# Two transformer blocks on one core: GpSimd's part of the first block's mixer given to other engines, and late vectors loaded by another queue

## The chip, the cores and the metric

The program runs on one core of a Trainium2 chip. The metric is device time in microseconds (us) for one execution; the median of three runs of the kernel before is 3050.2 us (3048.06 to 3050.91). The engines are named as in the profile: PE is TensorE, DVE is VectorE, ACT is ScalarE, POOL is GpSimd, SP is SyncE; SPq and ACTq are the issues of DMAs by SP and ACT.

## The reference

Two blocks run one behind the other over x (256 tokens) and a context ctx (256 tokens) of 1024 columns, all in f32, each block with two layers. A layer of the first block is a feed-forward half step, a mixer, and another feed-forward half step, each behind an RMS norm whose shift and scale come from an adaLN product with c. The mixer, cut to what the change touches:

```python
q = rms_norm((rms_norm(q_lat, g_q_lat) @ w_q_up).reshape(b, n, 8, 96), g_q_head)
k = rms_norm(concat([k_nope, k_pe]), g_k_head)      # 64 + 32 columns a head
q, k = apply_rope(q, rope), apply_rope(k, rope)     # on the last 32; not for ctx
attn = softmax(q @ k.T * 96 ** -0.5) @ v            # x attends to x and ctx, ctx to ctx

u, v = split(gelu(sg_in)); v = rms_norm(v, g_sgu)   # 4 groups of 64 columns
sg = u * (einsum('gpq,bnqgc->bnpgc', w_spatial, v) + b_spatial)

cv = b_gate * conv3(c_gate * xin, w_conv)           # three taps along the tokens
h = h + gate * (concat([norm(attn), norm(sg), norm(cv)]) @ w_mix_out)
```

In layer 1, the last of the block, ctx needs keys and values alone. The second block's code is the same before and after.

## The kernel before, in words

Activations lie feature-major in SBUF: 128 features by 512 tokens, x as tokens 0 to 255 (stream 0), ctx as 256 to 511 (stream 1). Every weight is loaded as f32 by SP (`load_raw`, L301, tile `wr`, three buffers) and split into a high part by ACT (`wh`, L310) and a low part by DVE (`wl`, L311); activations are split in the same way (`xnh` by L593, `xnl` by L594; `gh`, `ysh` and others by L590, low parts by L591). A product is three matmuls, high by high, low by high, high by low (L340 to L342 feature-major, L354 to L356 token-major). A scheduler of the framework fixes the order of the instructions on each engine at build time; on the chip each engine then runs its own list in order and waits by semaphore.

**Start.** x and ctx are transposed to feature-major. `Sumsq.add` squares the eight tiles of a stream (ACT L95, L98) and sums them (DVE L100, the last by L103); PE sums over features (L548, psum `nm`), DVE makes the reciprocal root (L559 to L567), PE spreads it (L542). The first adaLN chunk is loaded by SP as eight tiles `ar` (L156, 1 MB each) in four parts; PE multiplies them (L167) and each part frees two of the eight feature tiles to be normed (DVE L133, ACT L593, DVE L594). `first_pair` of `ffn` multiplies them as they come (psum `fa`), so its four parts run one behind the other. The weights of the first pair are `wr_285` and `wr_293`, of the second `wr_655` and `wr_663`. After the second pair of layer 0, `load_vectors` is called for the vectors that are wanted later: 14 small DMAs into `rows` (L405), a transpose on PE (L409) and a copy to `cols` (L410). They are issued by ACT.

**Mixer 1** (`mixer1`). Constants come into one buffer `blk` by ACT's queue (L916 to L925): rope tables, the two head gains (broadcast to all partitions; the query's is scaled on POOL, L920), the gain `gsgu`, the bias `sgb`. Latents are projected and normed (`rms_split`; of its tiles every second low part is done by POOL, L591). Then come the gate's values `vg` (gelu, L878 to L883), the queries `qraw` and keys `kraw` (token-major, 128 tokens by 2 by 8 heads by 96), with sums of squares per head in `qss` and `kss` (16 columns each, two of either), and the shared rope part of the keys, which POOL copies to all heads (L1016). `head_scale` is called for each stream's queries and keys: a reciprocal root of 16 columns in eleven small DVE steps (L854, L527 to L531), a multiply by it (DVE L859), a multiply by the gain (POOL L860), and, for stream 0, rope per group of 128 tokens: L866, four small rotations L870 and L871, a sum L872. Beside this the projections for `yB` (gelu) and the short convolution (L1032, L1038 to L1041) run; `gating` transposes `w_spatial` (L1058, copied to `sg` by L1059) and norms `vg` (L1061 to L1070, its last two multiplies on POOL). POOL clears the unused 32 partitions of `qT` and `kT` (L1096). For each head PE then transposes keys and queries (L1101, psum `tr`), which ACT (L1103) and DVE (L1105) copy to `kT` and `qT`. Attention follows, in steps: scores (PE L804), maximum (DVE L810), exp (ACT L812), scaling (DVE L814, L815), transposes (PE L825) and values (L835).

## Time and profile before

| | us |
|---|---|
| median of 3 runs | 3050.2 |
| profiled execution, its own time | 3051.59 |
| its span | 3049.9 |
| PE busy | 2927.8 (96%) |
| DVE busy | 2151.0 (71%) |
| ACT busy | 1083.4 (36%) |
| POOL busy | 130.1 (4%) |
| mean granted clock of PE | 0.979 |

The profiled execution is a single one with its own time beside its span. Each instruction in it has a start and a length, and for idle time before it the profile names what ended the wait. PE's clock is a share of its full speed; it has two levels, 0.50 (1.2 GHz) and 1.00 (2.4 GHz), and a window shows the mean. Shares of the whole span average over stages with different limits, so the places around an edit are read by windows and by rows of single engines.

### The profile page before, as it was taken

To read this page: it belongs to the slowest core of one execution; us is meant where nothing else is said; L and a number is where in the kernel's file an instruction comes from. 1 tells how busy PE (TensorE), PEld (TensorE's weight loads), DVE (VectorE), ACT (ScalarE), POOL (GpSimd) and SP (SyncE) were. 2 spreads that over 40 slices of the span, in tenths; PEclk is the share of its full clock that TensorE was granted. 3 is DMA by queue.
4 is the path that set the end of the run, shared out by engine and by line. 5 is a ranking of instruction groups with operands and counts; after the bars stand their busy time and mean duration, and the time that the engine had idled before them with its cause. 6 is when DMAs were issued, how large, how long until landed. Compare 5 with 4: busy or idle time off the path is not lost.

```text
span 3049.9 us, 44489 instructions
## 1 busy us (share of the span) xinstructions
PE 2927.8 (96%) x17770; PEld 2489.2 (82%) x17770; DVE 2151.0 (71%) x4361; ACT 1083.4 (36%) x1977; POOL 130.1 (4%) x138
## 2 busy tenths in 40 slices
PE   5999999999999999999978999999999999999998
PEld 4788889678788888878857999886887879886998
DVE  4887868968887688877796575337688875536665
ACT  2222235443222232222544444235432223434443
POOL 0000001300000000000030000011000000011000
PEclk7999999999999999999989999999999999999999
DMA  6555533204655445554322554201245552312553
GB/s 224 171 193 185 174 100 95 75 15 157 203 193 165 152 138 188 185 193 145 101 93 70 182 182 136 74 7 53 80 156 174 186 189 62 113 51 69 164 180 111
DMA packets 357571, 410.52 MB, mean 135 GB/s; under 512 B 23774, under 2 KB 297844, under 8 KB 357364
## 3 DMA queue, kind: packets, MB, share of 16 engines
q1 hardware_dynamic: 353040, 403.48, 41.0%
q10 hardware_dynamic: 4324, 4.20, 0.4%
q8 instruction: 140, 2.29, 0.3%
q14 instruction: 67, 0.55, 0.1%
HBM read 406.60 MB, written 1.05 MB: 134 GB/s over the span
## 4 chain that ended last, share of the span: by engine, by line
PE 89%; DVE 7%; DMA 2%; ACT 1%; issue 1%; SPq 0%; POOL 0%; ACTq 0%; DVEq 0%; POOLq 0%
PE pj L340 13%; PE pj L341 12%; PE pj L342 12%; PE fa L340 9%; PE fa L341 9%; PE fa L342 9%; PE po L835 2%; PE pf L340 2%; PE pf L342 2%; PE pf L341 2%; PE sc L804 2%; DVE wl L311 2%; PE pt L825 1%; PE ada L483 1%; PE pj L354 1%; PE pj L355 1%
## 5 line engine op out<-in xcount | busy, mean ns | idle before, releaser
L310 ACT ACTIVATE wh<-wr 128x1024 fp32r<-128x1024 f32 (+3 forms) x542 | 525.9, 1017 | 877.1 <-PE pj L341 470.6
L311 DVE TENSOR_TENSOR wl<-wr,wh 128x1024 fp32r<-128x1024 f32 (+3 forms) x542 | 629.9, 1184 | 171.3 <-ACT wh L310 169.5
L472 DVE SCALAR_TENSOR_TENSOR ad<-wr,silu,ad 128x512 f32<-128x512 f32 x784 | 551.2, 750 | 16.5 <-DMA wr<-in_w_ada_dram 16.5
L340 PE MATMUL fa<-xnh,wh 128*128 128x512 f32 (+1 forms) x1472 | 519.6, 360 | 6.3 <-ACT xnh L593 4.5
L341 PE MATMUL fa<-xnl,wh 128*128 128x512 f32 (+1 forms) x1472 | 522.5, 357 | 2.0 <-DVE xnl L594 2.0
L342 PE MATMUL fa<-xnh,wl 128*128 128x512 f32 (+1 forms) x1472 | 522.6, 357 | 0.9 <-DVE wl L311 0.9
L340 PE MATMUL pj<-gh,wh 128*128 128x256 f32 (+1 forms) x1372 | 458.9, 336 | 0.0
L342 PE MATMUL pj<-gh,wl 128*128 128x256 f32 (+1 forms) x1372 | 456.8, 333 | 0.0
L341 PE MATMUL pj<-gl,wh 128*128 128x256 f32 (+1 forms) x1372 | 456.2, 333 | 0.0
L340 PEld LDWEIGHTS fa<-xnh,wh 128*128 128x128 f32 x1472 | 275.5, 189 | 53.2 <-issue 7.8
L342 PEld LDWEIGHTS fa<-xnh,wl 128*128 128x128 f32 x1472 | 277.8, 189 | 43.6 <-DVE wl L311 1.4
L341 PEld LDWEIGHTS fa<-xnl,wh 128*128 128x128 f32 x1472 | 277.5, 189 | 43.2 <-DVE xnl L594 3.2
L340 PEld LDWEIGHTS pj<-gh,wh 128*128 128x128 f32 x1372 | 258.6, 189 | 30.6 <-issue 4.0
L342 PEld LDWEIGHTS pj<-gh,wl 128*128 128x128 f32 x1372 | 258.2, 188 | 27.3
L341 PEld LDWEIGHTS pj<-gl,wh 128*128 128x128 f32 x1372 | 258.8, 189 | 26.2 <-issue 0.4
L341 PE MATMUL pj<-xnl,wh 128*128 128x256 f32 (+1 forms) x824 | 260.5, 320 | 1.2 <-DVE xnl L594 1.0
L340 PE MATMUL pj<-xnh,wh 128*128 128x256 f32 (+1 forms) x824 | 259.1, 324 | 2.4 <-ACT xnh L593 2.2
L342 PE MATMUL pj<-xnh,wl 128*128 128x256 f32 (+1 forms) x824 | 261.0, 320 | 0.0
L340 PEld LDWEIGHTS pj<-xnh,wh 128*128 128x128 f32 x824 | 155.1, 192 | 15.6 <-ACT xnh L593 3.2
L341 PEld LDWEIGHTS pj<-xnl,wh 128*128 128x128 f32 x824 | 156.6, 191 | 13.0 <-DVE xnl L594 1.7
L342 PEld LDWEIGHTS pj<-xnh,wl 128*128 128x128 f32 x824 | 156.3, 190 | 11.6
L686 DVE SCALAR_TENSOR_TENSOR h<-pj,gate,h 128x256 f32<-128x256 f32 x168 | 75.8, 481 | 99.2 <-PE pj L342 99.0
(373 smaller groups left out, 4387.9 us busy)
## 6 DMA issues: line engine op xcount, KB each, us to landing
wr<-in_w_ada_dram SPq DMA_DIRECT2D x112, 1024.0 KB, 5.2
wr<-in_w_ffn_in_dram SPq DMA_DIRECT2D x88, 1024.0 KB, 5.1
wr<-in_w_mlp_dram SPq DMA_DIRECT2D x64, 1024.0 KB, 5.5
...
```

The lines of the kernel that those rows point to most:

```text
L310: self.nc.scalar.activation(h[:, i0:i1], raw[:, i0:i1], AF.Copy)
L311: self.nc.vector.tensor_tensor(l[:, i0:i1], raw[:, i0:i1], h[:, i0:i1].bitcast(F32), op=ALU.subtract)
L340: nc.tensor.matmul(o, wh, x.H(k, c0, c1), start=st, stop=False)
L341: nc.tensor.matmul(o, wh, x.L(k, c0, c1), start=False, stop=False)
L342: nc.tensor.matmul(o, wl, x.H(k, c0, c1), start=False, stop=en)
L354: nc.tensor.matmul(ps_ap, xh, w.h[:, kw, n0:n1], start=st, stop=False)
L355: nc.tensor.matmul(ps_ap, xh, w.l[:, kw, n0:n1], start=False, stop=False)
L472: nc.vector.scalar_tensor_tensor(acc[:, j], raw[:, k - k0], s[:, k, j : j + 1], acc[:, j], op0=ALU.mult, op1=ALU.add)
L483: nc.tensor.matmul(ps[q : q + 32, :P], self.sumto[:, 3 - r : 35 - r], acc[:, j, o : o + P], start=(r == 0), stop=(r == 3), tile_position=( ...
L686: self.nc.vector.scalar_tensor_tensor(self.h[m][:, e0:e1], ps[:, e0 - c0 : e1 - c0], gate[:, m, s : s + 1], self.h[m][:, e0:e1], op0=ALU.m ...
L804: nc.tensor.matmul(ps[:, :w], q_ap(q0), k_ap(k0 * P, (k0 + nk) * P), start=True, stop=bias is None)
L835: nc.tensor.matmul(o, v_ap(k0 + k), pT[:, k, :], start=(k == 0), stop=(k == nk - 1), tile_position=(0, 64 * j))
```

## The change

It does four things. In `ffn`, the late vectors' DMAs are issued by SP instead of ACT, with `g_sgu` as one more of them. In `head_scale`, the gains go: those of the rope columns into tables made once per mixer (`head_table`), those of the other 64 into a column `gcol` by which the evacuations of the transposes multiply; all 16 (token group, head) pairs are done by one instruction, and the roots of both streams by one chain of 32 columns (`rms`). gelu leaves out its halving (`gelu2`, with the factors in `gsc`, `sgb` and the norm's mean). And POOL's remaining work in the mixer goes to DVE (low parts, the `vg` norm) or ACT (the copies of the rope part), or is no longer needed (the clearing; transposes now take 128 columns from a flat raw tile of 1568, and 128 partitions are evacuated). ACT also gets the convolution's first tap.

```diff
@@ setup, ffn @@
-             ("g_q_lat", a["g_q_lat"]), ("g_kv_lat", a["g_kv_lat"]), ("g_out", a["g_out"]), ("w_conv", a["w_conv"])],
+             ("g_q_lat", a["g_q_lat"]), ("g_kv_lat", a["g_kv_lat"]), ("g_out", a["g_out"]), ("w_conv", a["w_conv"]), ("g_sgu", a["g_sgu"])],
...
-                    self.load_vectors(2, len(self.groups), nc.scalar)
+                    self.load_vectors(2, len(self.groups), nc.sync)
@@ split_from, rms_split @@
-        eng = nc.gpsimd if pool else nc.vector
...
-            eng.tensor_tensor(l, t, h.bitcast(F32), op=ALU.subtract)
+            nc.vector.tensor_tensor(l, t, h.bitcast(F32), op=ALU.subtract)
...
-                self.split_from(u, dst, k0 + i, c0, c1, pool=i % 2 == 1)
+                self.split_from(u, dst, k0 + i, c0, c1)
@@ head_scale, head_table, gelu2: the new bodies @@
+    def head_scale(self, raw, y, tab):
+        v = self.nc.vector
+        r = raw.rearrange("p t h d -> p (t h) d")
+        v.tensor_tensor(r, r, y.unsqueeze(2).broadcast_to([P, 16, 96]), op=ALU.mult)
+        pe = raw[:, :, :, 64:96]
+        if len(tab.shape) == 2:
+            pe = r[:, :, 64:96]
+            v.tensor_tensor(pe, pe, tab.unsqueeze(1).broadcast_to([P, 16, 32]), op=ALU.mult)
+            return
...
+        v.tensor_tensor(t1, pe, tab[:, 0].unsqueeze(2).broadcast_to([P, 2, 8, 32]), op=ALU.mult)
         for t in range(2):
+            for o in (0, 8):
...
+                v.tensor_tensor(dst, src, sn.unsqueeze(1).broadcast_to([P, 8, 2, 8]), op=ALU.mult)
+        v.tensor_tensor(pe, t1, t2, op=ALU.add)
+    def head_table(self, tab, g):
+        v = self.nc.vector
+        v.tensor_tensor(tab[:, 0], self.cosq, g.unsqueeze(1).broadcast_to([P, 2, 32]), op=ALU.mult)
+        for t in range(2):
+            half = lambda ap, o: ap.rearrange("p (a b) -> p a b", b=16)[:, :, o : o + 8]
+            v.scalar_tensor_tensor(half(tab[:, 1, t], 0), half(self.sinq[:, t], 0), -1.0, half(g, 8), op0=ALU.mult, op1=ALU.mult)
+            v.tensor_tensor(half(tab[:, 1, t], 8), half(self.sinq[:, t], 8), half(g, 0), op=ALU.mult)
+    def gelu2(self, out, x_ps, w):
...
+        nc.scalar.activation(sq, x_ps, AF.Square, scale=float(np.sqrt(0.044715)))
+        nc.vector.scalar_tensor_tensor(sq, sq, 1.0, x_ps, op0=ALU.add, op1=ALU.mult)
         nc.scalar.activation(sq, sq, AF.Tanh, scale=float(np.sqrt(2.0 / np.pi)))
+        nc.vector.scalar_tensor_tensor(out, sq, 1.0, x_ps, op0=ALU.add, op1=ALU.mult)
@@ mixer1: constants @@
-        nc.gpsimd.tensor_scalar(gbc[:, 0:96], gbc[:, 0:96], 96 ** -0.5, None, op0=ALU.mult)
-        nc.scalar.dma_start(gsgu, a["g_sgu"][l].rearrange("g c -> (g c)").unsqueeze(0).broadcast_to([P, 256]))
+        for i, nm in enumerate(("g_q_head", "g_k_head")):
+            nc.scalar.dma_start(gcol[:64, i : i + 1], a[nm][l, 0:64].unsqueeze(1))
+        v.memset(gcol[64:96], 1.0)
+        v.memset(gcol[96:], 0.0)
+        v.tensor_scalar(gcol[:64, 0:1], gcol[:64, 0:1], 96 ** -0.5, None, op0=ALU.mult)
+        v.tensor_scalar(gbc[:, 64:96], gbc[:, 64:96], 96 ** -0.5, None, op0=ALU.mult)
+        for i in range(2):
+            self.head_table(tabs[i], gbc[:, 96 * i + 64 : 96 * i + 96])
+        v.tensor_scalar(gsc, self.vec("g_sgu", 2 * l, 2), 0.25, None, op0=ALU.mult)
...
+        v.tensor_scalar(sgb, sgb, 0.5, None, op0=ALU.mult)
@@ mixer1: heads @@
+            flat = self.arena([P, 1568], F32, name)
+            v.memset(flat[:, 1536:], 0.0)
...
+        def rms(ss, n):
+            v.tensor_scalar(ss[:, :n], ss[:, :n], 1.0 / 96, EPS, op0=ALU.mult, op1=ALU.add)
+            y = self.small(32, "hy")
+            self.rsqrt_small(y[:, :n], ss[:, :n], n)
...
-            nc.gpsimd.tensor_copy(kraw[tt // 2][:, tt % 2, :, 64:96], kpe[:, tt, :].unsqueeze(1).broadcast_to([P, 8, 32]))
+            nc.scalar.activation(kraw[tt // 2][:, tt % 2, :, 64:96], kpe[:, tt, :].unsqueeze(1).broadcast_to([P, 8, 32]), AF.Copy)
+        kst = kss.rearrange("p (t h) -> p t h", h=8)
+        v.tensor_tensor(kst, kst, pes.unsqueeze(2).broadcast_to([P, 4, 8]), op=ALU.add)
+        yq = rms(qss, 8 * nt)
+        yk = rms(kss, 32)
         for s in range(2):
             if s < len(streams):
-                self.head_scale(qraw[s], qss[s], gbc[:, 0:96], s == 0)
-            self.head_scale(kraw[s], kss[s], gbc[:, 96:192], s == 0)
+                self.head_scale(qraw[s], yq[:, 16 * s : 16 * s + 16], gbc[:, 64:96] if s else tabs[0])
+            self.head_scale(kraw[s], yk[:, 16 * s : 16 * s + 16], gbc[:, 160:192] if s else tabs[1])
@@ mixer1: convolution, gating, transposes @@
-            v.tensor_scalar(yy, zz, wc(1), None, op0=ALU.mult)
+            nc.scalar.activation(yy, zz, AF.Copy, scale=wc(1))
...
-            nc.gpsimd.tensor_tensor(vgs, vgs, yv[:, : nt * 4].unsqueeze(2).broadcast_to([P, nt * 4, 64]), op=ALU.mult)
-            nc.gpsimd.tensor_tensor(vg[:, :nt, :], vg[:, :nt, :], gsgu.unsqueeze(1).broadcast_to([P, nt, 256]), op=ALU.mult)
+            v.tensor_tensor(vgs, vgs, yv[:, : nt * 4].unsqueeze(2).broadcast_to([P, nt * 4, 64]), op=ALU.mult)
...
-        for t_ in qT + kT:
-            nc.gpsimd.memset(t_[96:, :, :], 0.0)
...
+                    nc.tensor.transpose(ps[:, tt * P : (tt + 1) * P], src[tt // 2][:, o : o + P], self.ident)
+                if src is kflat:
+                    nc.scalar.activation(dst[h // 4][:, h % 4, : n * P], ps[:, : n * P], AF.Copy, scale=gcol[:, 1:2])
                 else:
+                    v.tensor_scalar(dst[h // 4][:, h % 4, : n * P], ps[:, : n * P], gcol[:, 0:1], None, op0=ALU.mult)
```

Three places where the scheduler's order comes out otherwise follow. In rows of the changed kernel, line numbers are those of its own file; `sq` and `acc` are the squares and their sum, `h` the tiles of x and ctx.

The first is ACT at the start, among the squares; rows with a minus stood there before, rows with a plus stand there now.

```order
 L98 ACTIVATE sq_167<-h_97 128x256
-L405 DMA rows<-in_norm_g_dram 16x128 x2
-L405 DMA rows<-in_mlstm_norm_g_dram 8x128
 L98 ACTIVATE sq_211<-h_92 128x256
-L405 DMA rows<-in_final_g_dram 8x128
 L98 ACTIVATE sq_218<-h_93 128x256
 L98 ACTIVATE sq_225<-h_94 128x256
 L98 ACTIVATE sq_232<-h_95 128x256
-L310 ACTIVATE wh_287<-wr_285 128x1024 x2
 L98 ACTIVATE sq_239<-h_96 128x256
 L98 ACTIVATE sq_246<-h_97 128x256
```

The vectors' DMAs are gone from between ctx's squares (tiles `sq_211` to `sq_246`), and the split of the first weight, `wh_287`, now follows all of them. Somewhat later ACT's list has, now as before (where the line is L593), the tiles of part 1 of the first norm with the split of the second pair's weight among them:

```order
L592 ACTIVATE xnh_359<-nt_439,mod_104 128x256
L592 ACTIVATE xnh_359<-nt_443,mod_104 128x256
L592 ACTIVATE xnh_359<-nt_447,mod_104 128x256
L310 ACTIVATE wh_657<-wr_655 128x1024 x2
L592 ACTIVATE xnh_359<-nt_451,mod_104 128x256
```

The last tile of part 1 (`nt_451`) stands behind `wh_657` in both.

The second is SP at the start, behind the load `wr_655`; the first six of the added rows are left out.

```order
+L405 DMA rows<-in_g_out_dram 16x128
+L405 DMA rows<-in_w_conv_dram 12x128
+L405 DMA rows<-in_g_sgu_dram 4x128
+L405 DMA rows<-in_b_ada_dram 72x128
+L405 DMA rows<-in_b_ada_dram 96x128
+L405 DMA rows<-in_norm_g_dram 16x128 x2
+L405 DMA rows<-in_mlstm_norm_g_dram 8x128
+L405 DMA rows<-in_final_g_dram 8x128
 L301 DMA wr_663<-in_w_ffn_in_dram 128x8x256
 L301 DMA wr_723<-in_w_ada_dram 128x4x512
```

All 15 vector loads stand between the two weights of the second pair; nothing else of SP's list moves there.

The third is DVE in layer 1's mixer, up to the first evacuation of a query's transposes (`tr` to `qT`). Before:

```order
L879 TENSOR_SCALAR gq_12901<-gq_12901 128x256
L872 TENSOR_TENSOR kraw_12631<-rope_12802 128x8x32
L1064 TENSOR_REDUCE vm_13102<-vsq_13103 128x4
L872 TENSOR_TENSOR kraw_12631<-rope_12811 128x8x32
L880 TENSOR_TENSOR gq_12869<-gq_12869,pj_12844 128x256
L880 TENSOR_TENSOR gq_12901<-gq_12901,pj_12876 128x256
L1064 TENSOR_REDUCE vm_13102<-vsq_13106 128x4
L882 SCALAR_TENSOR_TENSOR gq_12869<-gq_12869,pj_12844 128x256
L1065 TENSOR_SCALAR vm_13102<-vm_13102 128x8
L882 SCALAR_TENSOR_TENSOR gq_12901<-gq_12901,pj_12876 128x256
L883 TENSOR_SCALAR yB_12835<-gq_12869 128x256
L1105 COPY qT_13124<-tr_13138 96x256
```

Now:

```order
L1096 TENSOR_REDUCE vm_13018<-vsq_13019 128x4
L1072 SCALAR_TENSOR_TENSOR yB_12755<-vgz_12392,cols,yB_12755 128x255
L1071 SCALAR_TENSOR_TENSOR yB_12755<-vgz_12392,cols,yB_12755 128x255
L869 TENSOR_TENSOR kraw_12590<-rope_12745,rope_12746 128x16x32
L1091 COPY sg_13010<-wsT_13012 128x512
L311 TENSOR_TENSOR wl_13683<-wr_13680,wh_13682 128x1024 x2
L887 SCALAR_TENSOR_TENSOR yB_12755<-gq_12789,pj_12764 128x256
L887 SCALAR_TENSOR_TENSOR yB_12755<-gq_12819,pj_12794 128x256
L1073 TENSOR_TENSOR yB_12755<-yB_12755,pj_12952 128x256
L1096 TENSOR_REDUCE vm_13018<-vsq_13022 128x4
L1072 SCALAR_TENSOR_TENSOR yB_12755<-vgz_12392,cols,yB_12755 128x255
L1135 TENSOR_SCALAR qT_13039<-tr_13049,blk_12054 128x256
```

The rope sum of the keys (L872 before, L869 now) has moved ahead of most of gelu's and the gating's steps, L879 and L883 are gone, and two pieces of a weight (`wl_13683`) now stand between that sum and the first evacuation.

## Rows read from the trace of the kernel before

**Rows 1.** Page, part 1: busy time, share of the span, instructions of each engine

```profile
PE 2927.8 (96%) x17770; PEld 2489.2 (82%) x17770; DVE 2151.0 (71%) x4361; ACT 1083.4 (36%) x1977; POOL 130.1 (4%) x138
```

**Rows 2.** Waits of PE (what waited <- for what: us, times, longest)

```profile
PE nm L548 <- DVE acc L100: 30.7, 4, 24.9
PE tr L1101 <- DVE kraw L872: 20.7, 1, 20.7
...
PE tr L1101 <- DVE yB L1041: 5.3, 2, 3.4
```

**Rows 3.** Windows: length; busy PE, PEld, DVE, ACT, POOL; clock, DMA share, GB/s

```profile
20.00:25.00 5.00, 0.00 (x0) 0.00 (x0) 0.00 (x0) 0.00 (x0) 0.00 (x0) 0.50 1.10 347
...
200.00:440.00 240.00, 240.00 (x1264) 196.65 (x1263) 177.01 (x287) 59.12 (x82) 0.00 (x0) 1.00 0.49 162
...
560.00:570.00 10.00, 3.96 (x24) 2.97 (x23) 9.86 (x17) 2.89 (x4) 6.44 (x4) 0.80 0.34 105
...
580.00:600.00 20.00, 18.95 (x109) 11.67 (x106) 16.90 (x58) 13.70 (x36) 1.18 (x2) 1.00 0.27 75
...
1560.00:1570.00 10.00, 0.00 (x0) 0.00 (x0) 10.00 (x12) 0.00 (x0) 9.44 (x5) 0.50 0.33 105
```

**Rows 4.** Timeline, ACT: start, length, engine, line, work [idle before <-releaser]

```profile
16.80 17.63 ACTq L405 DMA_DIRECT2D rows<-in_norm_g_dram  x2
34.47 0.34 ACTq L405 DMA_DIRECT2D rows<-in_mlstm_norm_g_dram  x1
34.85 0.42 ACT L98 ACTIVATE sq<-h 128x256 f32<-128x256 f32 x1 [18.48 <-DMA ar<-in_w_ada_dram]
...
64.03 1.99 ACT L310 ACTIVATE wh<-wr 128x1024 fp32r<-128x1024 f32 x2
65.92 0.50 ACT L593 ACTIVATE xnh<-nt,mod 128x256 fp32r<-128x256 f32 x1
...
91.69 2.01 ACT L310 ACTIVATE wh<-wr 128x1024 fp32r<-128x1024 f32 x2 [0.46 <-PE fa L342]
```

**Rows 5.** Timeline, PE: the first fa matmul; in layers 0 and 1

```profile
53.33 1.48 PE L340 MATMUL fa<-xnh,wh 128*128 128x512 f32 x4
...
561.57 0.60 PE L1101 MATMUL tr<-ident,qraw 128*96 128x128 f32 x4
562.01 0.60 PE L1101 MATMUL tr<-ident,kraw 128*96 128x128 f32 x4
...
576.50 2.74 PE L804 MATMUL sc<-kT,qT 128*128 128x512 f32 x6
...
1578.80 1.45 PE L804 MATMUL sc<-kT,qT 128*128 128x512 f32 x3
```

**Rows 6.** Timeline, SP's DMA issues

```profile
31.27 11.36 SPq L301 DMA_DIRECT2D wr<-in_w_ffn_in_dram  x2
```

**Rows 7.** Windows at the start, columns as in rows 3

```profile
41.00:42.00 1.00, 0.00 (x0) 0.00 (x0) 1.00 (x3) 1.00 (x3) 0.00 (x0) 0.50 0.38 118
...
50.00:55.00 5.00, 5.00 (x42) 3.99 (x39) 2.33 (x6) 1.30 (x3) 0.00 (x0) 0.60 0.05 19
...
110.00:120.00 10.00, 9.04 (x56) 7.19 (x55) 10.00 (x18) 3.25 (x4) 2.54 (x1) 1.00 0.80 232
```

**Rows 8.** Timeline, POOL, layer 1's mixer

```profile
1560.50 5.43 POOL L860 TENSOR_TENSOR kraw<-kraw,blk 128x768 f32<-128x768 f32 x2 [4.74 <-DVE kraw L859]
```

**Rows 9.** Timeline, DVE, layer 1's mixer

```profile
1536.32 2.87 DVE L311 TENSOR_TENSOR wl<-wr,wh 128x1024 fp32r<-128x1024 f32 x1
...
1540.85 0.16 DVE L530 SCALAR_TENSOR_TENSOR nt<-nt,hy 128x16 f32<-128x16 f32 x1
...
1550.76 1.81 DVE L530 SCALAR_TENSOR_TENSOR nt<-nt,hy 128x16 f32<-128x16 f32 x1
...
1566.35 3.49 DVE L879 TENSOR_SCALAR gq<-gq 128x256 f32<-128x256 f32 x2
...
1573.41 0.40 DVE L1105 COPY qT<-tr 96x256 f32<-96x256 f32 x1
```

More of the change, by code (lines that the diff above doesn't have):

```diff
@@ L581, in sumsq, with split_from @@
         return [acc]
-    def split_from(self, t, dst, k, c0, c1, bias=None, pool=False):
+    def split_from(self, t, dst, k, c0, c1, bias=None):
         nc = self.nc
@@ L874, in gelu @@
-    def gelu(self, out, x_ps, w):
+    def head_scale(self, raw, y, tab):
[7 more added lines that the diff above has]
+            return
+        t1 = self.tmp(T, "rope").rearrange("p (t h d) -> p t h d", t=2, h=8)
+        t2 = self.tmp(T, "rope").rearrange("p (t h d) -> p t h d", t=2, h=8)
+        v.tensor_tensor(t1, pe, tab[:, 0].unsqueeze(2).broadcast_to([P, 2, 8, 32]), op=ALU.mult)
+        for t in range(2):
+            for o in (0, 8):
+                dst = t2[:, t].rearrange("p h (a b) -> p h a b", b=16)[:, :, :, o : o + 8]
+                src = pe[:, t].rearrange("p h (a b) -> p h a b", b=16)[:, :, :, 8 - o : 16 - o]
+                sn = tab[:, 1, t].rearrange("p (a b) -> p a b", b=16)[:, :, o : o + 8]
+                v.tensor_tensor(dst, src, sn.unsqueeze(1).broadcast_to([P, 8, 2, 8]), op=ALU.mult)
+        v.tensor_tensor(pe, t1, t2, op=ALU.add)
@@ L883, in gelu @@
-        nc.vector.tensor_scalar(out, sq, 0.5, None, op0=ALU.mult)
+        nc.vector.scalar_tensor_tensor(out, sq, 1.0, x_ps, op0=ALU.add, op1=ALU.mult)
     def rms_split(self, tiles, n, gcol, dst, k0, streams):
@@ L913, in mixer1 @@
         self.sinq = blk[:, 256:320].rearrange("p (t d) -> p t d", d=32)
-        gsgu = blk[:, 320:576]
+        tabs = [blk[:, 320 + 128 * i : 448 + 128 * i].rearrange("p (c t d) -> p c t d", c=2, t=2) for i in range(2)]
         sgb = blk[:, 576:832].rearrange("p (g q) -> p g q", q=P)
+        gcol = blk[:, 832:834]
+        gsc = blk[:, 834:836]
         nc.scalar.dma_start(self.cosq, a["rope1"][0].rearrange("(t p) d -> p t d", p=P))
@@ L981, in mixer1, with heads @@
             if tt in tts:
-                self.gelu(vg[:, tt, :], pvk[tt][:, 32:288], 256)
-        qraw = [self.arena([P, 2, 8, 96], F32, "qraw") for _ in range(len(streams))]
-        qss = [self.small(16, "qss") for _ in range(2)]
+                self.gelu2(vg[:, tt, :], pvk[tt][:, 32:288], 256)
+        def heads(name):
+            flat = self.arena([P, 1568], F32, name)
+            v.memset(flat[:, 1536:], 0.0)
+            return flat, flat[:, :1536].rearrange("p (t h d) -> p t h d", t=2, h=8)
+        def rms(ss, n):
+            v.tensor_scalar(ss[:, :n], ss[:, :n], 1.0 / 96, EPS, op0=ALU.mult, op1=ALU.add)
+            y = self.small(32, "hy")
+            self.rsqrt_small(y[:, :n], ss[:, :n], n)
+            return y
+        qflat, qraw = zip(*[heads("qraw") for _ in range(len(streams))])
+        qss = self.small(32, "qss")
         for half in range(2):
@@ L995, in mixer1 @@
                 nc.scalar.activation(sq, ps[:, :384], AF.Square)
-                o = (tt % 2) * 8 + 4 * half
-                v.tensor_reduce(qss[tt // 2][:, o : o + 4], sq.rearrange("p (h d) -> p h d", d=96), axis=AX.X, op=ALU.add)
-        kraw = [self.arena([P, 2, 8, 96], F32, "kraw") for _ in range(2)]
-        kss = [self.small(16, "kss") for _ in range(2)]
+                o = tt * 8 + 4 * half
+                v.tensor_reduce(qss[:, o : o + 4], sq.rearrange("p (h d) -> p h d", d=96), axis=AX.X, op=ALU.add)
+        kflat, kraw = zip(*[heads("kraw") for _ in range(2)])
+        kss = self.small(32, "kss")
         vt = self.arena([P, 4, 512], F32, "vt")
@@ L1025, in mixer1 @@
         self.project([(w, [0, P], None)], x, streams, False, range(KT),
-                     lambda tag, j, ps, e0, e1: self.gelu(yB[:, j, e0:e1], ps[:, : e1 - e0], e1 - e0))
+                     lambda tag, j, ps, e0, e1: self.gelu2(yB[:, j, e0:e1], ps[:, : e1 - e0], e1 - e0))
         def ev_c(tag, j, ps, e0, e1):
@@ L1094, in mixer1 @@
         kT = [self.arena([P, 4, T], F32, "kT") for _ in range(2)]
[L1095 to L1096 removed]
         for h in range(8):
[L1098 removed]
+            for src, dst, n in ((kflat, kT, 4), (qflat, qT, nt)):
                 ps = self.psum("tr")
                 for tt in range(n):
[L1101 to L1103 removed]
+                    o = (8 * (tt % 2) + h) * 96
+                    nc.tensor.transpose(ps[:, tt * P : (tt + 1) * P], src[tt // 2][:, o : o + P], self.ident)
+                if src is kflat:
+                    nc.scalar.activation(dst[h // 4][:, h % 4, : n * P], ps[:, : n * P], AF.Copy, scale=gcol[:, 1:2])
                 else:
[L1105 removed]
+                    v.tensor_scalar(dst[h // 4][:, h % 4, : n * P], ps[:, : n * P], gcol[:, 0:1], None, op0=ALU.mult)
         yA = self.arena([P, 4, T], F32, "yA")
```

41 lines of the change are left out of this document (5 added, 36 removed).

## The prediction

> **What bounds the kernel now.** The page comes first: TensorE (PE) is busy for 2927.8 us, 96% of the span [rows 1]. An edit can only save time in the remaining 122 us, or by having PE run at full clock sooner. The list of PE's waits says where those are: one of 24.9 us (30.7 in four) for VectorE's (DVE's) sums at L548, one of 20.7 us at the transposes L1101 for the keys that DVE's L872 writes, and two of 5.3 us in sum at the same transposes [rows 2]. All three places are touched. The windows give their surroundings [rows 3]: at 20 to 25 us PE, DVE, ScalarE (ACT) and GpSimd (POOL) all do nothing while the DMA engines move 347 GB/s, and PE's granted clock is 0.50, its lower level; at 200 to 440 us PE is busy for 240 of 240 us beside DVE's 177; at 1560 to 1570 us PE does nothing while DVE works for all of 10 us beside 9.44 of POOL. What is won at the start is kept, since the long stretch behind it is bound by PE.
>
> **The wait at the start.** ACT squares x and ctx at L98, but its order mixes the 14 DMA issues of `load_vectors` into that. Two issues of the norm gains take 17.63 us from the first's start to the second's end, while SP fills the DMA engines with 1 MB loads, and the next square comes after 18.48 us of idleness [rows 4]. DVE's adds and PE's L548 hang on it. The change takes these issues out of ACT's order, so ctx's last six squares can follow at about 17 us. At 0.42 us at most [rows 4] they are done by 20 us; the reciprocal roots and the norm follow, and I put the first `fa` matmul at about 25 us, where it was 53.33 [rows 5].
>
> That is not a gain of 28 us, since the next thing is late. In ACT's order, which the change keeps there, the split `wh_657` of the third feed-forward weight (wr_655) stands ahead of the last `xnh` tile of part 1: at 64.03 and 65.92 us before [rows 4]. wr_655 is issued behind eight adaLN loads, at 31.27 us [rows 6], and the DMA rate falls to 118 GB/s in 41 to 42 us [rows 7], so it lands at 41.4 to 43 us; I take 42.3. With 1.99 us of ACT for the split, the last tile starts at 44.3 instead of 65.92: 21.6 us sooner. PE comes to it after idleness, at its lower clock: the stretch 50 to 55 us shows what that costs, a granted 0.60 over 5 us, or 2 to 2.5 us of full-speed work [rows 7]. **Start term: 21.6 − 2.5 = 19 us.** Bounds: 14 if PE pauses again in parts 2 and 3; 28 (53.33 − 25) if wr_655 does not hold it.
>
> On SP, 15 small issues (the 14 and `g_sgu`) now stand between wr_655 and wr_663. An undisturbed issue takes 0.34 us [rows 4], so 5 us in sum; wr_663 is split only after the first pair's first evacuation, at 91.69 us before [rows 4], some 72 now. I count this at nothing; its bad case is a rival. The Trainium skill, "DMA: Bandwidth & Descriptors", "Issuing engines are not separate DMA queues", says that DMAs of any issuing engine share the same 16 engines and that another issuer only saves the sequencer's issue time, usually small. This speaks against the move: by it ACT would get back about 14 × 0.34 = 5 us. The trace does not bear it out here: two issues held ACT for 17.63 us, and my sum goes by that row.
>
> **Mixer 1, layer 1.** DVE falls behind PE here, because its instructions are held while POOL multiplies by the head gains (L860, 5.43 us for the last two [rows 8]). The same 128x16 step of a reciprocal root (L530) takes 1.81 us beside such a multiply and 0.16 without [rows 9]. From 1536 to 1570 us I count seven rows so lengthened (L311, L531, L530, L1040, L866, L870 and the pair L879), by 1.65, 1.66, 1.65, 1.55, 1.28, 1.61 and 2.81 us over their usual lengths: 12.2 in sum; the first, third and last stand in [rows 9]. With no POOL work in the mixer they go. DVE's own list becomes shorter too: L879 and L883 fall out of gelu (four of a 128x256 operation's 0.40 us [rows 9]), root chains of 16 columns merge into chains of 32, the sixteen rotations of 64 elements for q and k become eight of 128; some 3 us together. The first `qT` evacuation, which ends PE's real waiting, moves from 1573.41 [rows 9] to about 1558. The transposes behind it still start from the lower clock, so the first scores move by the same 15 us, from 1578.80 [rows 5] to 1563.8. **Term: 15 us.** Lower bound 10: the new order still has weight pieces L311 and the gating's sums ahead of that evacuation. Upper bound 18: the wait of 20.7 us [rows 2] but for the work that stays.
>
> **Mixer 1, layer 0.** PE's waits are shorter (the two for yB, 5.3 us [rows 2]), but clock is lost too: 0.80 in 560 to 570 us, with DVE busy for 9.86 and POOL for 6.44 of 10 us [rows 3]. Undisturbed, a group of four transposes takes a step of 0.44 us (561.57 to 562.01 [rows 5]). Sixteen groups from 560.2 are 7.0 us, so scores could start at 567.2 instead of 576.50 [rows 5]. **Term: 9.3 us**; bounds 5 (the two waits alone) and 10.
>
> **What it adds.** (1) Some 20 small DVE operations per mixer for the tables, at 0.16 us like L530's undisturbed row [rows 9]: 3 us each time. In layer 0 they stand among the adaLN products near 110 to 120 us, where DVE is busy throughout and PE for 9.04 of 10 [rows 7]: −1.5. Layer 1's stand in layer 0's attention, behind DMAs that cannot be issued before the constants' one buffer is free; DVE, busy for 16.90 of 20 us there beside PE's 18.95 [rows 3], waits some microseconds for them. (2) Twelve `ysl` low parts come from POOL to DVE at 0.40 us (a 128x256 operation [rows 9]), eight of them in that attention: 3.2 us. What POOL held DVE there falls away. For both together I take −3 (bounds 0 and −6). (3) ACT gets the kpe copies, a conv tap and scales inside evacuations: it does nothing in 1560 to 1570 us [rows 3], so this costs nothing while ACT waits for PE there. (4) Transposes of 128 instead of 96 columns and evacuations of 128 partitions: as many instructions, nothing.
>
> The sum is 19 + 15 + 9.3 − 1.5 − 3 = 39 us against the profiled execution's own 3051.6: 3012.6. The median of the runs lies 1.4 us lower, so **3011 us**.
>
> **Rivals.**
> - **The start gains only 5 us**: ACT's long issue was only the shared DMA engines at work, and something else that lands late holds the norm. For it: ACT's wait ends with an adaLN load's landing [rows 4]. Against: the squares need only x and ctx, which DVE copies from the transposes before. Then 39 − 14 = 25: 3026. It is also the time by the skill's rule above. Chance 0.08.
> - **The start is not held by wr_655** and gains 28 to 30 us: 3000. The order of ACT speaks against it. Chance 0.10.
> - **The mixers give back half** (12 of their 24 us), because DVE, with table steps and `ysl` parts, comes late in the attentions: 3023. For it: DVE's 16.90 of 20 us [rows 3]. Against: POOL's holds leave that stretch as well. Chance 0.12.
> - **Slower: the 15 issues block SP as two blocked ACT.** At 17.63 / 2 = 8.8 us each, 132 in sum, wr_663 goes out at about 34 (a load's issue after 31.27 [rows 6]) + 132 = 166 us and every weight behind it waits. It decides once an issue takes over (72 − 34) / 15 = 2.5 us. PE would stall for 166 − 72 = 94 us; less the 39 won, +55: 3105. For it: the same kind of issue beside the same loads [rows 4]. Against: only wr_655 is in flight by then, and by 42 us the DMA rate has fallen [rows 7]. Chance 0.03.
> - **Nothing measurable**: what PE waited for was not what the change frees. 3045 to 3056; chance 0.03.
>
> **How the numbers follow.** The forecast case has 0.64, with 3003 to 3021 by its own bounds. To hold 8 in 10 the range takes in the unheld start and both smaller gains: 2998 to 3028. About 0.2%, 6 us, is what a measurement tells from no change: faster 0.94, same 0.03, slower 0.03.
>
> **What would show it.** Right: ACT's squares end before 21 us; PE's wait at L548 is under 3 us; PE pauses once and resumes at 43 to 46 us, behind the split of wr_655; no 16- or 32-column DVE row over 0.3 us in the mixers; PE's wait at the transposes is under 6 us in layer 1; in layer 0 scores follow the last projection within 8 us. Wrong: SP spends over 40 us on the issues behind wr_655 and PE waits for L310; POOL rows in the mixers; PE waits at L825 of over 5 us in sum in the attentions.

## The result, and the profile after

The changed kernel takes **3011.1 us** (median of four runs, 3000.9 to 3016.5) beside 3049.7 for the kernel before on the same chip (four runs, 3048.1 to 3050.9): ratio 0.9863, 95% interval 0.9847 to 0.9879 (the two medians alone give 0.987). The forecast was 3011, range 2998 to 3028. Of the four runs the profiled one is the slowest: 3016.51 us, span 3014.8, at a mean granted clock of 0.984; the fastest had 0.989. 0.005 of 3000 us is 15 us, about as much as the four runs scatter (15.7), so small differences are read below as shifts: the same matmul is found in two traces, and how much earlier it starts, from each span's start, is compared from place to place. Of the four executions of e0 below one took 11555 us and is left out.

The page's first part, as in [rows 1], then PE's waits, as in [rows 2]:

```profile
PE 2933.0 (97%) x17770; PEld 2491.0 (83%) x17770; DVE 2123.1 (70%) x4322; ACT 1088.8 (36%) x1989; POOL 47.5 (2%) x83
```

```profile
PE nm L542 <- DVE rs L567: 22.1, 9, 4.6
PE nm L548 <- DVE acc L100: 7.8, 4, 4.1
...
PE tr L1131 <- DVE kraw L869: 3.3, 1, 3.3
```

PE does the same 17770 matmuls. POOL loses 83 us of work. The wait of 20.7 us at the transposes [rows 2] is 3.3. That of 24.9 us at L548 is 1.79 (21.54 below); the 4.1 in this list stands behind layer 1's attention (1617 us), where the kernel before has 4.3.

**The start.** ACT's timeline, as in [rows 4]; PE's follows. Columns are start, length, engine, line, work, and in brackets the idle time before with what ended it.

```profile
19.60 0.42 ACT L98 ACTIVATE sq<-h 128x256 f32<-128x256 f32 x1 [2.65 <-DVE acc L100]
20.32 0.42 ACT L98 ACTIVATE sq<-h 128x256 f32<-128x256 f32 x1 [0.31 <-DVE acc L100]
20.65 3.88 ACT L310 ACTIVATE wh<-wr 128x1024 fp32r<-128x1024 f32 x4
...
42.80 1.31 ACT L592 ACTIVATE xnh<-nt,mod 128x256 fp32r<-128x256 f32 x3 [10.55 <-DVE nt L133]
44.01 1.99 ACT L310 ACTIVATE wh<-wr 128x1024 fp32r<-128x1024 f32 x2
45.90 0.49 ACT L592 ACTIVATE xnh<-nt,mod 128x256 fp32r<-128x256 f32 x1
```

```profile
21.54 0.61 PE L548 MATMUL nm<-sumto,acc 128*128 128x1 f32 x4 [1.79 <-DVE acc L100]
...
29.16 1.22 PE L542 MATMUL nm<-ident,rs 128*128 128x128 f32 x4 [4.60 <-DVE rs L567]
...
33.60 1.19 PE L340 MATMUL fa<-xnh,wh 128*128 128x512 f32 x4
```

The squares end at 20.74 us, and L548 comes 21.7 us earlier than before (43.23). The first `fa` comes at 33.60, 19.7 us earlier [rows 5], but not at 25: between its norm sum and its broadcast L542 stand 4.60 us in which PE waits for DVE's `rs`. DVE's timeline shows with what it is busy there: with four low parts of the first two weights, which stand in its order among the steps of the reciprocal root.

```profile
22.00 1.22 DVE L311 TENSOR_TENSOR wl<-wr,wh 128x1024 fp32r<-128x1024 f32 x1
23.13 0.15 DVE L567 SCALAR_TENSOR_TENSOR rs<-nt,rs 128x2 f32<-128x2 f32 x1
23.20 1.22 DVE L311 TENSOR_TENSOR wl<-wr,wh 128x1024 fp32r<-128x1024 f32 x1
...
24.41 1.22 DVE L311 TENSOR_TENSOR wl<-wr,wh 128x1024 fp32r<-128x1024 f32 x1
...
26.00 1.22 DVE L311 TENSOR_TENSOR wl<-wr,wh 128x1024 fp32r<-128x1024 f32 x1
```

The split of wr_655 (44.01 in ACT's rows) starts right behind the tiles ahead of it, which had waited 10.55 us for DVE: it waits for no landing. The last tile comes at 45.90, 20.0 us earlier than its 65.92 [rows 4]. SP's 15 small issues hold nothing up: they stand between wr_655 and wr_663, 12.4 us in all,

```profile
32.61 2.25 SPq L405 DMA_DIRECT2D rows<-in_c_dram  x1
34.91 0.30 SPq L405 DMA_DIRECT2D rows<-in_c_ctx_dram  x1
...
44.60 0.29 SPq L405 DMA_DIRECT2D rows<-in_final_g_dram  x1
44.99 0.39 SPq L301 DMA_DIRECT2D wr<-in_w_ffn_in_dram  x1
```

and wr_663 (44.99) is first split at 71.58.

**The mixers.** PE in layer 0, from the weights' transposes (L1090, 559.72 before) to the first scores, then the same in layer 1 (1549.06 before); compare [rows 5]:

```profile
540.56 0.60 PE L1090 MATMUL wsT<-ident,sg 128*128 128x128 f32 x4
541.00 0.60 PE L1131 MATMUL tr<-ident,kraw 128*128 128x128 f32 x4
...
548.38 1.88 PE L803 MATMUL sc<-kT,qT 128*128 128x512 f32 x4
```

```profile
1525.32 0.60 PE L1090 MATMUL wsT<-ident,sg 128*128 128x128 f32 x4
1529.23 1.11 PE L1131 MATMUL tr<-ident,kraw 128*128 128x128 f32 x4 [3.32 <-DVE kraw L869]
...
1540.03 2.74 PE L803 MATMUL sc<-kT,qT 128*128 128x512 f32 x6
```

Layer 0's sixteen groups run without a gap at 0.44 us each; from L1090 to the scores it takes 7.8 us instead of 16.8. In layer 1 it takes 14.7 instead of 29.7: PE waits 3.32 us, and twice more for 0.78 and 0.62, and transposes mostly at its lower clock (0.57 granted; a window, columns as in [rows 3]):

```profile
1530.00:1540.00 10.00, 8.60 (x46) 7.86 (x45) 9.21 (x27) 4.73 (x7) 0.00 (x0) 0.57 0.40 127
```

How much earlier than in the trace of before, at places named by their time in that trace; the second column is the changed kernel run once more (e0):

| place | after | e0 | forecast |
| --- | --- | --- | --- |
| first `fa`, 53 us | 19.7 | 22.0 | |
| end of layer 0's projections, 540 | 19.2 | 19.5 | 19 − 1.5 |
| layer 0's scores, 576.5 | 28.1 | 28.5 | + 9.3 |
| out of attention 0, 671 | 26.1 | 26.9 | − 3 |
| layer 1's weight transposes, 1549 | 23.7 | 25.1 | |
| layer 1's scores, 1578.8 | 38.8 | 40.7 | + 15 |
| behind attention 1, 1660 | 35.0 | 40.1 | |
| span's end | 35.1 | 37.6 | 39 |

Some 1.5 us of the shift at 1660 are not the change's: every trace, that of e1 with the old mixers too, gains them between 1627 and 1635 us.

### The profile page after: what moved, and what is told of

The parts are those of the page before. It is cut to its first block, busy times and chain, and to the rows that moved or that the text cites. A ratio compares the mean times of both kernels' runs of the same rounds, so it can differ in the third digit from the quotient of the medians.

```text
span 3014.8 us, 44377 instructions
## 1 busy us (share of the span) xinstructions
PE 2933.0 (97%) x17770; PEld 2491.0 (83%) x17770; DVE 2123.1 (70%) x4322; ACT 1088.8 (36%) x1989; POOL 47.5 (2%) x83
## 4 chain that ended last, share of the span: by engine, by line
PE 91%; DVE 5%; DMA 1%; ACT 1%; issue 1%; SPq 0%; POOL 0%; ACTq 0%; DVEq 0%; POOLq 0%
PE pj L340 13%; PE pj L341 13%; PE pj L342 13%; PE fa L340 9%; PE fa L341 9%; PE fa L342 9%; PE po L834 3%; PE pf L340 2%; PE pf L342 2%; PE pf L341 2%; PE sc L803 2%; DVE wl L311 2%; PE pj L354 1%; PE ada L483 1%; PE pj L355 1%; PE pj L356 1%
```

## The experiments

All ran beside the kernel before on the same chip; times are medians. That kernel's own medians lay between 3050.4 and 3059.0 us in these rounds, so each ratio is to the runs beside it, and kernels of different rounds are compared by ratio or by shift.

**e1: the queue alone.** The kernel before, with one word changed.

```diff
-                    self.load_vectors(2, len(self.groups), nc.scalar)
+                    self.load_vectors(2, len(self.groups), nc.sync)
```

> The kernel before with one word changed: the 14 late-vector DMAs are issued by SP instead of ACT; the mixers stay as they were. Theory (ACT's squares stood behind the issues): ACT's squares of ctx end before 22 us, PE's wait of 24.9 us at L548 shrinks to about 4, the first fa matmul comes near 33.6 us as in the changed kernel, and the whole is shorter by 19 to 20 us, some 3030. Rival (only the issue time is saved, the DMA engines are shared): shorter by 5, some 3045. The mixers' waits (20.7 us at the transposes in layer 1) stay in both.

3037.6 us, ratio 0.9932 (0.9908 to 0.9956): 21 us less. L542 moves from 48.62 to 27.67, and the shift stays between 19 and 23 us up to 2720. The profiled execution lost half of it again there, far from the edit: behind a wait of 1.2 us PE is busy, at half the clock, for three windows (the first and last; columns as in [rows 3]).

```profile
2730.00:2740.00 10.00, 10.00 (x37) 8.28 (x36) 5.73 (x23) 2.22 (x7) 2.21 (x4) 0.50 0.00 0
...
2750.00:2760.00 10.00, 10.00 (x36) 7.96 (x34) 4.24 (x15) 2.65 (x7) 0.79 (x1) 0.50 0.01 2
```

So the start term belongs to the queue alone.

**e2: the mixer alone.** The changed kernel with the same word put back.

```diff
-                    self.load_vectors(2, len(self.groups), nc.sync)
+                    self.load_vectors(2, len(self.groups), nc.scalar)
```

> The changed kernel with the late vectors put back on ACT's queue. Theory (the parts are independent): the start is again late by about 20 us (first fa matmul near 53 us), the mixers keep their gain of 9 and 15 us less some 7 given back in the attentions, so some 3030, 19 to 20 under the time before. Rival (the mixers' gain depends on the start, or the start's on the mixers): the difference to the time before is under 10 or over 28.

3030.8 us, ratio 0.9913 (0.9879 to 0.9948). Layer 0's mixer gives 9.0 us and layer 1's 16.7, at the same places as in the changed kernel. Where layer 0's tables stand (112 us) its shift changes by 0.04 us only. The parts are independent as far as the intervals tell: the ratios of e1 and e2 multiply to 0.985, that of both is 0.986.

**e8: the issues stay on ACT, behind the last square of ctx.**

```diff
...
-                    self.load_vectors(2, len(self.groups), nc.scalar)
+                    with self.tc.issue_after(self.start_sq.ins):
+                        self.load_vectors(2, len(self.groups), nc.scalar)
```

> The kernel before with the 14 issues left on ACT's queue, but ordered behind the last square of ctx. Theory (what counts is what stands behind the issues on ACT): the first sums at L548 are as early as in the changed kernel, near 22 us; but the issues now stand between the splits of the first weights and the first xnh tiles, so if each blocked issue costs ACT up to 9 us while the adaLN loads fill the queue, the first fa matmul comes at 40 to 45 us instead of 33.6, and the gain is 8 to 13 instead of 20. Rival (the queue itself matters, not the order): no gain over the time before, first fa matmul near 53.

3054.9 us, ratio 0.9987 (0.9964 to 1.001): nothing gained, where 8 to 13 us were expected. L548 is early (19.72 us) but ctx's L542 is not (47.09). ACT's timeline comes first:

```profile
24.98 0.28 ACTq L405 DMA_DIRECT2D rows<-in_c_ctx_dram  x1
27.98 0.32 ACTq L405 DMA_DIRECT2D rows<-in_g_mix_dram  x1
...
37.38 2.00 ACT L310 ACTIVATE wh<-wr 128x1024 fp32r<-128x1024 f32 x2 [13.02 <-DMA ar<-in_w_ada_dram]
...
44.78 0.51 ACT L593 ACTIVATE xnh<-nt,mod 128x256 fp32r<-128x256 f32 x1 [5.40 <-DMA rows<-in_g_out_dram]
```

Issues go out once in 3.0 us, until 43 us, and then one in 0.4; the weight pieces and the tile behind them wait. 3.0 us is what a 1 MB load takes at the 347 GB/s of [rows 3]. DVE passes the delay on to PE: the low parts among the steps of its root wait for ACT's high parts.

```profile
38.47 1.23 DVE L311 TENSOR_TENSOR wl<-wr,wh 128x1024 fp32r<-128x1024 f32 x1 [12.52 <-ACT wh L310]
```

```profile
47.09 1.22 PE L542 MATMUL nm<-ident,rs 128*128 128x128 f32 x4 [21.08 <-DVE rs L567]
```

So behind the squares the issues still stand ahead of work that the norm needs. That no place on ACT would do is not shown: one behind the splits and the first tiles, or this one with the low parts moved as in e6, was not tried. Why an issue on ACT takes 3.0 us is open too: on SP, from 34.9 to 36.7 us in the changed kernel, five take 0.3 to 0.4 us each while the DMA engines move 385 GB/s (35 to 36 us).

**e0: the changed kernel again**, unedited.

> The changed kernel once more. Its four runs lay between 3001 and 3017 with mean granted clocks of 0.989 to 0.984. Theory (the scatter is PE's clock alone): each run's span minus its best is the span times its clock's difference, 3 us for every 0.001, and a trace shows stretches of half clock in other places, while the shifts against the trace before in the start and in the mixers stay at 20, 9 and 15 us within 1. Rival (the scatter is DMA landing times or queue order): clocks agree and the start or the mixers move.

3011.2 us (three runs), ratio 0.9844 (0.9793 to 0.9895). The terms come again (table above).

**e4: POOL's multiplies come back, as work that nobody waits for.** For each call of `head_scale` two multiplies of 128x768 on a scratch tile, which depend on the root alone.

```diff
...
+        for t in range(2):
+            sc = self.scr.rearrange("p (h d) -> p h d", d=96)
+            self.nc.gpsimd.tensor_tensor(sc, sc, y[:, 8 * t : 8 * t + 8].unsqueeze(2).broadcast_to([P, 8, 96]), op=ALU.mult)
```

> The changed kernel with idle work added on POOL: in each head_scale two multiplies of a scratch tile of 128x768 by the roots, 14 in all, as the gains' multiplies were, but on data that no other engine reads or waits for. Theory (DVE's instructions are held while POOL reads, whatever it reads): DVE rows of 32 columns or 768 elements show again 1.6 to 1.7 us more beside them, some 12 to 14 of them, and of the 24 to 26 us that the two mixers gained 9 to 19 are lost again, most of it in layer 1. Rival (the keys' way through POOL was the cost, DVE waiting for POOL's results): no DVE row is longer, the loss is under 2 us.

One time, 3011.8. DVE's rows in layer 1 beside POOL's, then the first transposes:

```profile
1508.32 1.46 DVE L530 SCALAR_TENSOR_TENSOR nt<-nt,hy 128x32 f32<-128x32 f32 x1
...
1510.84 1.96 DVE L867 TENSOR_TENSOR rope<-qraw,blk 128x512 f32<-128x512 f32 x1
...
1518.82 4.71 DVE L859 TENSOR_TENSOR kraw<-kraw,hy 128x1536 f32<-128x1536 f32 x2
```

```profile
1506.73 5.51 POOL L858 TENSOR_TENSOR scr<-scr,hy 128x768 f32<-128x768 f32 x2 [981.41 <-DVE nt L529]
1518.92 9.41 POOL L858 TENSOR_TENSOR scr<-scr,hy 128x768 f32<-128x768 f32 x4 [6.68 <-DVE hy L531]
```

```profile
1534.39 1.11 PE L1136 MATMUL tr<-ident,kraw 128*128 128x128 f32 x4 [9.21 <-DVE kraw L874]
```

Without POOL the three DVE rows take 0.18, 0.69 and 3.43 us. Six rows of layer 1 are longer by 0.9 to 1.3 us each, 7.2 in sum, and the transposes come 5.2 us later than in the changed kernel (1529.23). Counted from the weights' transposes, the transposes of the heads lose 5.9 us (9.81 instead of 3.92) and the scores 4.8 (19.55 instead of 14.71). The holds are real. In layer 0, where seven rows are longer by 8.9 us in sum, DVE is mostly far enough ahead: from the weights' transposes to the scores it takes 9.1 us instead of 7.8, with two new waits of PE, 0.80 and 0.27 us.

```profile
543.49 0.66 PE L1136 MATMUL tr<-ident,qraw 128*128 128x128 f32 x4 [0.80 <-DVE qT L1140]
```

The expected size (9 us and more) was too high: some 6 us in both layers.

**e5: POOL only writes.** The multiplies replaced by 8 fills, behind a copy of one column.

```diff
...
+        self.nc.gpsimd.tensor_copy(self.scr[:, 0:1], y[:, 0:1])
+        for _ in range(8):
+            self.nc.gpsimd.memset(self.scr, 0.0)
```

> The changed kernel with idle work on POOL that only writes: in each head_scale eight fills of the same scratch tile of 128x768, some 5.5 us in all, started by one copy of a column of the roots. Theory (what holds DVE is POOL's reading): rows with two inputs from SBUF stay at their lengths, only copies and scalings may be held as L879 was beside the fills of qT; the mixers lose 0 to 4 us. Rival (any POOL work holds DVE): as with the reading kernel, 9 to 19 us.

One time, 3003.4; neither mixer loses anything. The one reading copy takes 1.73 us beside DVE's multiply of 1536 columns, and 0.18 at 1521.99 us, beside no such multiply. The fills run beside DVE, whose L867, with two inputs, takes its usual 0.68 us; but of DVE's rows with one input two are longer beside them in layer 0, by 0.4 and 0.6 us (the second below).

```profile
1502.83 1.73 POOL L856 COPY scr<-hy 128x1 f32<-128x1 f32 x1 [969.88 <-DVE hy L531]
1504.62 6.33 POOL L858 MEMSET scr<- 128x768 f32 x8
```

```profile
523.19 0.76 DVE L527 TENSOR_SCALAR vy<-vm 128x16 int32<-128x16 int32 x1
...
1505.93 0.68 DVE L867 TENSOR_TENSOR rope<-qraw,blk 128x512 f32<-128x512 f32 x1
```

The kernel before has a larger case of the second kind: its L879, with one input [rows 9], is held beside the fills of `qT`, the multiplies by the gains being over.

```profile
1565.99 3.69 POOL L1096 MEMSET qT<- 32x2048 f32 x2
```

So what holds DVE's rows with two inputs is POOL's reading. The Trainium skill, "SBUF — State Buffer", "Who interferes with whom", says so: a VectorE operation with two SBUF inputs contends with a GpSimd operation that reads SBUF, not with one that only writes it. The rows of e4 and e5 with two inputs agree.

**e6: the first weights' low parts behind the first norm tile.** On the changed kernel; the high parts stay where they are.

```diff
...
+                if i == 0:
+                    with self.tc.issue_after(self.xnl_end.ins):
+                        for i0, i1 in self.pieces(2048, 1024):
+                            for raw, (h_, l_) in zip(wr, hl):
+                                nc.vector.tensor_tensor(l_[:, i0:i1], raw[:, i0:i1], h_[:, i0:i1].bitcast(F32), op=ALU.subtract)
```

> The changed kernel with the low parts of the first two weights (four L311 pieces, 4 x 1.13 us) ordered on DVE behind part 0's norm instead of inside ctx's reciprocal root. Theory (the start is now bound by that root and, next, by the third weight's landing): L542 for ctx comes 4 to 4.5 us earlier, the first fa matmul near 29.5 instead of 33.6, but the last tile of part 1 waits on ACT for the split of wr_655, which can't begin before 41.4 us, so that tile starts at 43.4 to 44 instead of 45.9 and the first pair ends 2 us earlier. Rival (wr_655 is no bound): the pair ends 4 to 4.5 us earlier. Rival 2 (PE waits for the low parts instead): no gain.

3007.9 us, ratio 0.9845 (0.9818 to 0.9873). PE's and ACT's rows:

```profile
24.16 1.22 PE L542 MATMUL nm<-ident,rs 128*128 128x128 f32 x4 [2.96 <-DVE rs L567]
```

```profile
40.88 0.51 ACT L592 ACTIVATE xnh<-nt,mod 128x256 fp32r<-128x256 f32 x1 [0.66 <-DVE nt L133]
41.30 1.99 ACT L310 ACTIVATE wh<-wr 128x1024 fp32r<-128x1024 f32 x2
```

L542 comes 5.0 us earlier than in the first trace of the change, but 1.9 of that lie ahead of L548 (19.60 instead of 21.54; the unedited e0 has 19.61). From ctx's L548 to its L542 it takes 4.56 us instead of 7.62, so the four low parts cost 3.1. The last tile comes at 40.88 instead of 45.90; the new order also has it ahead of wr_655's split, which begins at 41.30 without a wait. So the low parts were the bound behind the queue, and wr_655's landing was none. The shift is 5 to 6 us ahead of the first trace and 3.6 to 5.3 ahead of e0 up to 671 us, beside the 2 us expected; the runs of one start differ by as much as 2.2 us at the first `fa`, and the times alone (0.9845 beside 0.9863, with overlapping intervals) don't tell the two kernels apart.

**e6b: e6, and the next pair's first split pinned behind part 3's last tile.**

```diff
...
-            ws = weights(t)
+            with self.tc.issue_after(self.xnh_end.ins) if start is not None and t == 2 else nullcontext():
+                ws = weights(t)
```

> As the kernel before it, and the split of the second pair's first weight ordered on ACT behind the last norm tile of part 3. Theory: with both holds gone the first pair ends 4 to 4.5 us earlier than in the changed kernel, and the second pair is not later for it, since its weight is split some 10 us before PE wants it; about 3007. Rival (the split now comes late): PE waits over 1 us for wh or wl of the second pair.

3012.1 us, ratio 0.9856 (0.9832 to 0.9881): of e6's 5 us only 0 to 2 are left behind 100 us. PE waits 1.98 us, at 61.30, for part 3's tiles, and restarts at its lower clock; in the changed kernel it runs on there, with a gap of 0.41. No wait for the late split itself shows. That PE lacked the second pair's matmuls there, because their weight is split only from 62.72 us, is likely but not shown. The pin cost what it was to save.

**e3: low parts of `ysl` on POOL again.** The condition caught six of the twelve, those of yB (four in layer 0, two in layer 1).

```diff
...
-                self.split_from(u, dst, k0 + i, c0, c1)
+                self.split_from(u, dst, k0 + i, c0, c1, pool=i % 2 == 1 and n == 256 and k0 >= 4)
```

> The changed kernel with one part undone: the twelve odd low parts of ysl (128x256 subtracts, eight in layer 0's attention, four in layer 1's) stand on GpSimd again. After the change attention 0 loses 2.5 to 3.2 us against the kernel before and attention 1 about 2 to 4. Theory A (these subtracts on VectorE are what is lost, 8 at 0.40 us): TensorE comes out of attention 0 about 2.5 us earlier than in the changed kernel and out of attention 1 about 1.5 us earlier; time 0.1% shorter, about 3008. Theory B (they fill gaps of VectorE; the tables and GpSimd's holds matter): nothing at either place, or a loss of up to 1 us, since a subtract on GpSimd reads two inputs and holds VectorE as the multiplies of e4 did; time within 3 us of the changed kernel but for the clock.

3006.1 us, ratio 0.9827 (0.9785 to 0.9869). Attention 0 loses 1.5 us from the scores to 671, as in e0 (1.6): no effect. In attention 1 three waits of PE, 0.53, 0.64 and 1.32 us in the changed kernel (first fence), become one of 0.18 (second), and 2.5 us of shift are kept:

```profile
1570.38 0.63 PE L824 MATMUL pt<-ident,p 128*128 128x128 f32 x4 [0.53 <-DVE p L814]
1577.47 0.63 PE L824 MATMUL pt<-ident,p 128*128 128x128 f32 x4 [0.64 <-ACT sq L579]
1579.41 1.03 PE L824 MATMUL pt<-ident,p 128*128 128x128 f32 x4 [1.32 <-DVE p L814]
```

```profile
1575.92 0.63 PE L825 MATMUL pt<-ident,p 128*128 128x128 f32 x4 [0.18 <-DVE p L815]
```

**e3b: all twelve**, with `(k0 >= 4 or n == 512)` in that condition.

> The changed kernel with all twelve odd low parts of ysl on GpSimd; the run before on this point moved six of them, those of yB (four in layer 0, two in layer 1), and gained nothing in attention 0 and 1.5 to 2.7 us in attention 1. Theory A (VectorE's time for them is what counts): the other six, of yA, behind the last heads of each stream, where TensorE waits for the norm, gain another 0.40 us at most at each stream's end, 1 us in all. Theory B (a read on GpSimd takes 0.7 us against 0.40 on VectorE and holds it): the six of yA lose up to 1 us instead. Time within 3 us of that run, 3003 to 3009, but for the clock.

3005.3 us, ratio 0.9831 (0.979 to 0.9873). Attention 0 loses 1.5 us and attention 1 gains 1.8, as in e3: the six of yA count neither way.

**e7: layer 1's constants and tables behind attention 0.** Their DMAs and their 20 small operations wait for its last exp.

```diff
...
+        with self.tc.issue_after(self.exp.ins) if l else nullcontext():
...
```

> The changed kernel with layer 1's constants and tables (its DMA issues and about 20 small VectorE operations) ordered behind the last exp of layer 0's attention, so that nothing of them stands inside it. Layer 0 stays as it is. Theory A (the tables are what attention 0 loses): TensorE comes out of attention 0 2 to 3 us earlier than in the changed kernel, keeps it to layer 1's mixer, and loses nothing there, since 800 us lie between. Theory B (the loss is that of the ysl parts or of a stretch at the lower clock): less than 1 us. Attention 1 has no tables behind it and stays the same under both.

3009.5 us, ratio 0.9835 (0.9785 to 0.9885). From the scores to 671 PE loses 0.3 us instead of 1.6. Theory A holds with half its size: in the changed kernel DVE's table steps at 557 to 562 us stand between two probabilities, and one waits for its DMA:

```profile
558.58 0.48 DVE L814 TENSOR_SCALAR p<-p,rinv 128x512 f32<-128x512 f32 x1
559.64 0.18 DVE L932 TENSOR_SCALAR blk<-blk 128x32 f32<-128x32 f32 x1 [0.58 <-DMA blk<-in_g_q_head_dram]
...
562.30 0.47 DVE L814 TENSOR_SCALAR p<-p,rinv 128x512 f32<-128x512 f32 x1
```

**c1: e6, e3 and e7 together.**

> Three edits on the changed kernel that gained by themselves, together: the two first weights' low parts behind the first norm tile (5 to 6 us), layer 1's constants and tables behind the last exp of layer 0's attention (1.3 us in the trace of that run), and the low parts of yB's odd tiles, six of the twelve, on GpSimd (nothing in attention 0, 1.5 to 2.7 us in attention 1). If the parts are independent, 8 to 9 us earlier than the changed kernel at the end, about 3002 at the same granted clock (0.985); TensorE then comes to layer 0's scores 33 to 34 us before the kernel before did, and out of attention 1 some 45 us before. Rival: low parts on GpSimd hold VectorE where it now comes earlier to the gating, and give back the 2 us: 3005.

3004.9 us (six runs, 3001.4 to 3012.1), ratio 0.9832 (0.9802 to 0.9861), against 0.9863 (0.9847 to 0.9879) for the change. Some 3002 us were expected, 8 to 9 less than the change. The two intervals overlap, so the times alone don't show that it is faster than the change. The trace has layer 0's scores 32.5 us earlier than before, and PE leaves attention 1 48.2 earlier, where e0 had 40.1. Some of that goes in later stretches at the lower clock: 44.6 at the end. It has the lowest median of the kernels with more than one time, but e3 and e3b lie within 1.2 us of it, which these runs can't tell apart.

## Why the prediction was right, and where its steps were wrong

**Start: 19 us, measured 19.8 behind the first pair (22.0 in e0), by another way.** The mechanism at L548 was right, and e1 shows it alone. Three steps behind it were wrong. The first `fa` came at 33.60, not 25: I counted ACT's squares and left DVE's order out, and four low parts of 1.22 us stood in it. wr_655's landing held nothing: the split ran without a wait in the changed kernel, and in e6, with the low parts moved, the last tile came 5.0 us earlier. And PE did not pause and resume at 43 to 46 us: it ran from 33.60 with gaps of 0.41 us at most. It had restarted once, from the lower clock (the window below), as the kernel before did at 50 to 55 us with 0.60 [rows 7]; this cost stood on both sides and was not to be taken off.

```profile
30.00:35.00 5.00, 5.00 (x44) 3.99 (x44) 2.45 (x6) 1.31 (x3) 0.00 (x0) 0.67 1.09 380
```

That 21.6 − 2.5 gave the right number was chance: the tile that I took as held by a load came 20.0 us earlier instead of 21.6 for what stood in DVE's order, and the 2.5 were nothing.

**SP's issues: nothing, and so it was.** They stood between wr_655 and wr_663 for 12.4 us, not 5, and wr_663 was out at 45.0, needed at 71.6. The slower rival would have needed 2.5 us for every issue; 0.8 is the mean.

**Mixer 1, layer 1: 15 us, measured 15.0 (15.6 in e0).** The sum fits, in part by two errors against each other. The first transposes of the heads came 17.3 us nearer to those of the weights, more than forecast; then they took 10.8 us to the scores instead of 8.5, with more of it at the lower clock and waits of 0.78 and 0.62 us inside. The working gave 12.2 us to POOL's multiplies by the gains, but 2.8 of these, L879's, stood beside POOL's fills. e4 brings 7.2 us of holds back and loses 4.8 at the scores (5.4 against e0); at that rate the 12.2 were worth some 8 to 9 (an estimate). The other 6 or 7 come from DVE's shorter list and its new order, which no run separates. PE's wait at the transposes is 3.3 us (forecast under 6).

**Mixer 1, layer 0: 9.3 us, measured 9.0.** From wsT to the scores 7.8 us, within the 8 named. Here e4 shows that the holds alone are worth 1.3 us; what went with them too, the multiplies of the gains in the chain itself, was not tried alone.

**What it adds: −4.5 us; measured −4.1 in e0, in other places.** Layer 0's tables cost next to nothing (0.04 us in e2), where I put 1.5 because DVE was busy throughout; e0's shift falls by 2.5 us there, but at a granted clock of 0.96 (85 to 125 us), and e1's, without tables, by 0.4. Attention 0 loses 1.6 us in e0 (2.0 in the first trace); most of it is the tables (1.3, e7) and not the `ysl` parts. In attention 1, which I gave nothing, the two odd parts of yB cost 2.5 us: between 1603 and 1619 us the shift falls by that in e0 and not at all in e3, e3b and c1 (in the first trace by 4.2, part of it at the lower clock). One sign of being wrong came out with this, just: PE's waits at L824 (L825 before) in the two attentions are 5.2 us in sum (1.9 before), where over 5 was named. Beyond the sum, 2.0 to 2.3 us go between 1120 and 1340 us in every trace with the new mixers and in none with the old ones (e1, e8), while PE is busy throughout at full clock; they are spread evenly over the `fa` matmuls. The cause is open.

**Rivals.** "Only 5 us" fell with e1: 21 us. It was also the time by the Trainium skill, "DMA: Bandwidth & Descriptors", "Issuing engines are not separate DMA queues": another issuing engine saves only the issue time, usually small. Here the issuer's time was not small, 3.0 us for an issue in e8. "Not held by wr_655" was right as to the mechanism, but not in its price of 28 to 30 us, since DVE came next; even with the low parts moved, in e6, the first `fa` came at 28.84, not 25. "Half given back" did not come.
